# Full precision products on half arrays in the attention of a streaming encoder step

## The chip, the cores and the metric

The kernel runs on one core of a Trainium2 chip. The metric is the device time of one execution in microseconds (us): median 2494.75 of three runs, 2488.86 to 2495.19. Everything is float32, and the result must agree with a float32 reference.

Names used below: PE is TensorE (matmuls; PEld its weight loads), DVE VectorE, ACT ScalarE, POOL GpSimd, SP the queue that issues nearly all DMAs. PSUM is the memory that PE writes, in banks of 2 KB for each of 128 partitions; SBUF is the working memory.

## The reference

One layer of an encoder, for a prompt of 2048 tokens and for 8 samples of 16 tokens. Cut to the part that the change touches, the attention of the prompt over its own and the two previous chunks of 64 keys (8 query heads, 2 key heads, 64 wide):

```python
def band_attend(q, k, v, mask, sinks):
    s = jnp.einsum('bnlkgd,bnskd->bnkgls', q, k, preferred_element_type=jnp.float32) * (A_HEAD_DIM ** -0.5)
    if mask is not None:
        s = jnp.where(mask, s, -jnp.inf)
    sink = sinks.astype(jnp.float32).reshape(A_KV_HEADS, A_GROUP)[None, None, :, :, None, None]
    mx = jnp.maximum(jnp.max(s, axis=-1, keepdims=True), sink)
    p = jnp.exp(s - mx)
    p = p / (jnp.sum(p, axis=-1, keepdims=True) + jnp.exp(sink - mx))
    o = jnp.einsum('bnkgls,bnskd->bnlkgd', p.astype(v.dtype), v, preferred_element_type=jnp.float32)
    return o.astype(v.dtype)

def trunk_layer(...):
    qm, km, vm, om, ip, fp, qa, ka, va = split_in(x @ w_in)
...
    hm, C1, n1, m1 = mlstm_chunkwise(qm, km, vm, logi, logf, C0, n0, m0, mchunk)
...
        ha = swa_prompt(qa, ka, va, attn_sinks)
...
    mix = jnp.concatenate([hm, ha], axis=-1) @ w_out
    h = layer_norm(DEEPNORM_ALPHA * x + mix, ln1_g, ln1_b)
    f, conv_rows = conv_ffn(h, conv_prev, w_up, w_conv, b_conv, w_down)
    y = layer_norm(DEEPNORM_ALPHA * h + f, ln2_g, ln2_b)
```

## The kernel before

The tokens are 17 tiles of 128: tiles 0 to 15 the prompt, tile 16 all samples. Work runs in three stages. First the input projection (`i_block`, five blocks of up to four tiles) and the output projection with the first norm (`o_block`); then the up projection with its convolution (`f_ups`); then the down projection (`f_downs`). The last two use a saving scheme of seven products for eight and aren't touched.

**Products in split form.** A PE product of the type float32r goes at full rate but keeps fewer bits. So most operands are split by `split` (line 200): ACT copies the value to a float32r tile (hi, line 202) and DVE subtracts it from the value (lo, line 203). `mm3` (line 205) then makes three products: hi x hi (line 207), hi x lo (208, 209). A product whose operands are float32 is made in full precision and appears in the trace as two matmul records.

**Chains between dense work.** The projections of blocks are dense streams of products of 512 or 264 columns (PSUM tile `dps`). The mLSTM, the attention and the sample tile are three chains (`m_chain`, `a_chain`, `t_sample`), written as generators. `Chains.weave` (line 170) walks through the dense stream and adds up its cost in ns; when a chain is due, it lets it issue its next piece. A piece ends with `yield cost, delay`: cost is what the piece adds to that sum, delay how much later the next piece is due. So the yields set the order of PE's instructions, which stands as written. The order of the other engines is made by the compiler's scheduler.

**The attention of a tile** (`swa`, line 782), before the change:

- `swa_load` (760) loads q (`qa`) and k with v (`kva`, one buffer), and transposes q and k on PE into the banks `pq` and `pk`.
- q, k and v are split (lines 790 to 792): `qh`/`ql`, `kringh`/`kringl`, and `vring`, which holds for each key head the 64 hi columns and the 64 lo columns of v beside each other. The rings hold three tiles of keys.
- Scores: a key head has its 64 dimensions on one half of PE's rows (partitions 0 to 63, or 64 to 127). For each key head in turn, and for two pairs of query heads (`j0`), a bank `psc` is filled by two times three products of 256 keys. DVE adds the mask and reduces to the maximum (`amx`, line 815), while copying to `sc`.
- Softmax: small DVE steps (817 to 824, `aes`, `asm`), eight exponentials on ACT (822), the division as a product on POOL (825).
- Values: per key head, the probabilities are transposed on PE (`ppt`, line 835), split into `pth` and `ptl`, and multiplied: the 128 columns hi and lo of `vring` as weights, `pth` and `ptl` as moving operand of 512 columns (lines 842, 843; bank `ppo`). ACT copies one half of `ppo` to `mixa` (845), DVE adds the other (846).

The mLSTM's pieces share PSUM with these: score bank `pscore` (672), key transposes `pkt` (683), gate banks `pe` (654, 664; read on ACT by `wi` and on DVE by `dt`), `pemt` (585), `pnum` and `pcu` (745 to 753), and `pht` (721), the transposed output, which ACT copies to `mixm` (723) after DVE, POOL and ACT have normed it (`hn`, `ms`).

**PSUM.** `self.bank` (line 483) takes from a pool of five banks (`tps`) for all three chains. A new tile waits on PE for the last reader of the bank that it is given. As PE's order is fixed, all that stands behind it in PE's queue waits too.

The sample's chain uses the tags `qh`, `ql`, `pth`, `ptl` for its own buffers.

Of the kernel before, what the change touches and what calls it, by code (L numbers as in the profile page):

```python
# [18 lines left out]
DB = 8  # L19
DS = 16  # L20
# [11 lines left out]
RING = 3  # L32
# [157 lines left out]
class Prog:  # L190
# [295 lines left out]
    def t_setup(self):  # L486
        nc, a, tp = self.nc, self.a, self.tp

        def ld(n):
            t = self.one("k_" + n, list(a[n].shape))  # L490
            nc.sync.dma_start(t, a[n])
            return t
        nc.sync.dma_start(self.ident, a["ident"])
        self.gb = ld("gb")
        self.mcau = ld("mcau")
        self.mblk = ld("mblk")
        self.mswa = ld("mswa")
# [284 lines left out]
    def swa(self, t):  # L782
# [21 lines left out]
        scs = []  # L804
        for kvh in range(2):
            rs = slice(64 * kvh, 64 * kvh + 64)
            sink = self.sink[:, 4 * kvh:4 * kvh + 4]
            sc = self.work("sc", [P, 4, 2 * P], bufs=2)
            mx, es, sm = [self.work(n, [P, 4], bufs=2) for n in ("amx", "aes", "asm")]
            for j0 in (0, 2):  # L810
                ps = self.bank([P, 2, 2, P], "psc")
                for j in range(2):
                    self.mm3(ps[:, j, :nk], qh[rs, j0 + j], ql[rs, j0 + j], self.kh[rs, sel], self.kl[rs, sel], True, True)
                for j in range(2):
                    V.tensor_tensor_reduce(out=sc[:, j0 + j, :N], in0=ps[:, j, :nk].rearrange("p a b -> p (a b)"), in1=mask, scale=1.0, scalar=-3e38,
                                           op0=ALU.add, op1=ALU.max, accum_out=mx[:, j0 + j:j0 + j + 1])
# [9 lines left out]
            scs.append(sc)  # L826
        yield 2600, 7500
        for kvh in range(2):
            rs = slice(64 * kvh, 64 * kvh + 64)
            sc = scs[kvh]  # L830
            pth, ptl = self.work("pth", [P, 2, 512], F32R), self.work("ptl", [P, 2, 512], F32R)
            for kt in range(nk):
                pp = self.bank([P, 512], "ppt")
                for j in range(4):
                    nc.tensor.transpose(pp[:, j * P:(j + 1) * P], sc[:, j, kt * P:(kt + 1) * P], self.ident)
                self.split(pth[:, kt], ptl[:, kt], pp)
            yield 860, 3000

            po = self.bank([P, 512], "ppo")
            for kt in range(nk):  # L840
                w = self.vv[:, slots[kt], kvh].rearrange("p a d -> p (a d)")
                nc.tensor.matmul(po, w, pth[:, kt], start=kt == 0, stop=False)
                nc.tensor.matmul(po, w, ptl[:, kt], start=False, stop=kt == nk - 1)
# [7 lines left out]
    def t_sample(self):  # L851
# [43 lines left out]
        for j in range(2):  # L895
            ps = self.bank([P, 2, 129], "pnum")
            for i in range(2):
                h = 2 * j + i
                cn = self.work(("pth", "ptl")[h % 2], [P, DB, 129], name="cns")
# [8 lines left out]
                for i3, b0 in enumerate((0, 3, 6)):  # L908
                    nb = min(3, DB - b0)
                    vw = self.work(("qh", "ql")[i3 % 2], [P, nb, 129], name="vws")  # L910
# [13 lines left out]
    def swa_sample(self):  # L924
# [6 lines left out]
        qs = self.work("qh", [P, DB, 64], name="qs")  # L931
        V.tensor_copy(qs.rearrange("p b (j l) -> p j b l", j=4), pq.rearrange("p j (b l) -> p j b l", b=DB))
        ks = self.work("ql", [P, P], name="ks")
# [6 lines left out]
        for half in range(2):  # L940
# [5 lines left out]
            vn = self.work("ptl", [DS, HB, P], name="vn")  # L946
# [23 lines left out]
            pts = self.work("pth", [P, 2, HB, P], name="pts")  # L970
# [560 lines left out]
```

## Time and profile before

| | us |
|---|---|
| median of three runs | 2494.75 |
| their lowest and highest | 2488.86, 2495.19 |
| the profiled execution | 2496.35 |
| its span, first to last instruction | 2494.6 |
| PE busy | 2395.8 (96%) |
| DVE busy | 1865.9 (75%) |
| ACT busy | 1205.2 (48%) |
| POOL busy | 467.2 (19%) |
| mean granted clock of PE | 0.984 |

The profile is of one execution. Times are from the start of the span. Matmuls are pipelined, and the end of one is modelled, so two records overlap; what a product costs in a stream is the time from its start to the next one's. "Idle before" or a wait names the engine that waited, and which instruction's end released it. The clock is the share of full speed that PE was granted.

The prompt's attention and mLSTM run from about 220 us to 910 us, woven into the projections; the sample tile comes before them, and the feed-forward part after some 1060 us.

### The profile page before, as it was taken

The page shows a single profiled execution, that of the slowest core. Times are in us where ns is not written, and L with a number is a line of the kernel's source. Part 1 is how long each engine was busy: PE and PEld are TensorE (multiplying, and loading weights), DVE is VectorE, ACT ScalarE, POOL GpSimd, SP SyncE. Part 2 cuts the span into 40 slices and gives each one's busy share as a digit, 9 for nine tenths or more (in the row PEclk, how much of TensorE's full clock was granted, in tenths as well). Part 3 has the DMA queues.
Part 4 walks back from the last instruction along what each step waited for, and adds up shares of the span by engine and source line. Part 5 has one row for each costly group of instructions (what it writes and reads, how often), then busy time and mean ns, then how long its engine had stood idle before and what let it go on. Part 6 is the DMA issues. An engine that isn't in the chain of part 4 may idle for free.

```text
span 2494.6 us, 36890 instructions
## 1 busy us (share of the span) xinstructions
PE 2395.8 (96%) x12922; PEld 2131.1 (85%) x12922; DVE 1865.9 (75%) x3244; ACT 1205.2 (48%) x2170; POOL 467.2 (19%) x486
## 2 busy tenths in 40 slices
PE   8999999999989899989999999999999999999998
PEld 8777778878887777789999999999999978778776
DVE  5656777487588887888788876678766677796897
ACT  4323445344355543555555545555544544444553
POOL 1211332132143434310000000002000010220300
PEclk9999999999998999999999999999999999999999
DMA  8886744544556567667777789886998876656653
GB/s 268 306 275 221 249 128 136 174 125 136 176 163 204 174 205 261 212 227 271 288 279 264 264 301 315 314 304 223 326 300 262 267 267 205 232 188 203 219 185 108
DMA packets 277117, 575.28 MB, mean 231 GB/s; under 512 B 45300, under 2 KB 122204, under 8 KB 276932
## 3 DMA queue, kind: packets, MB, share of 16 engines
q1 hardware_dynamic: 275204, 566.64, 67.3%
q0 software_dynamic: 1728, 6.29, 0.7%
q8 instruction: 102, 1.67, 0.3%
q14 instruction: 83, 0.68, 0.1%
HBM read 419.06 MB, written 153.78 MB: 230 GB/s over the span
## 4 chain that ended last, share of the span: by engine, by line
PE 54%; DVE 10%; issue 4%; DMA 3%; ACT 3%; POOL 2%; SPq 0%; DVEq 0%; ACTq 0%; POOLq 0%
PE dps L1240 16%; PE fup L1240 15%; PE fht L1437 5%; PE dps L1437 5%; PE fup L1437 5%; PE dps L207 2%; PE dps L209 2%; PE dps L208 2%; DVE wlo L203 2%; DMA zf<-cc 1%; ACT cc L1286 1%; DVE cc L1288 1%; DVE hl L203 1%; PE fht L1112 0%; POOL ymix L1028 0%
## 5 line engine op out<-in xcount | busy, mean ns | idle before, releaser
L1240 PE MATMUL fup<-hh,uw 128*128 128x384 f32 (+1 forms) x1848 | 483.6, 330 | 10.8 <-ACT u L1265 3.5
L1240 PE MATMUL dps<-hh,uw 128*128 128x384 f32 (+1 forms) x1848 | 481.7, 329 | 7.4 <-ACT u L1265 5.1
L203 DVE TENSOR_TENSOR wlo<-wraw,whi 128x1024 fp32r<-128x1024 f32 (+3 forms) x289 | 349.0, 1215 | 143.8 <-ACT whi L202 137.2
L202 ACT CAST whi<-wraw 128x1024 fp32r<-128x1024 f32 (+3 forms) x289 | 281.8, 981 | 310.4 <-PE dps L1437 94.0
L1240 PEld LDWEIGHTS fup<-hh,uw 128*128 128x128 f32 x1848 | 331.8, 189 | 13.9 <-ACT u L1265 4.7
L1240 PEld LDWEIGHTS dps<-hh,uw 128*128 128x128 f32 x1848 | 330.6, 188 | 9.6 <-ACT u L1265 6.6
L1288 DVE SCALAR_TENSOR_TENSOR cc<-u,cw,cc 128x768 f32<-128x768 f32 (+1 forms) x264 | 252.6, 977 | 110.6 <-ACT cc L1286 108.2
L207 PE MATMUL dps<-whi,xh 128*128 128x512 f32 (+1 forms) x816 | 317.3, 389 | 0.0
L209 PE MATMUL dps<-whi,xl 128*128 128x512 f32 (+1 forms) x816 | 310.5, 380 | 2.3 <-DVE xl L349 2.3
L208 PE MATMUL dps<-wlo,xh 128*128 128x512 f32 (+1 forms) x816 | 310.5, 380 | 2.1 <-DVE wlo L203 2.0
L1240 PE MATMUL fup<-hl,uw 128*128 128x384 f32 (+1 forms) x924 | 303.7, 329 | 1.4 <-DVE hl L203 1.4
L1240 PE MATMUL dps<-hl,uw 128*128 128x384 f32 (+1 forms) x924 | 302.7, 328 | 0.0
L1286 ACT ACTIVATE cc<-u,cw 128x768 f32<-128x768 f32 (+1 forms) x132 | 129.6, 997 | 117.7 <-DVE u L1279 58.1
L209 PEld LDWEIGHTS dps<-whi,xl 128*128 128x128 f32 x816 | 155.1, 190 | 34.1 <-DVE xl L349 2.7
L208 PEld LDWEIGHTS dps<-wlo,xh 128*128 128x128 f32 x816 | 155.7, 191 | 31.4 <-DVE wlo L203 2.9
L207 PEld LDWEIGHTS dps<-whi,xh 128*128 128x128 f32 x816 | 155.8, 191 | 30.1 <-ACT xh L348 0.4
L1240 PEld LDWEIGHTS fup<-hl,uw 128*128 128x128 f32 x924 | 174.4, 189 | 1.6 <-DVE hl L203 1.6
L1240 PEld LDWEIGHTS dps<-hl,uw 128*128 128x128 f32 x924 | 173.9, 188 | 0.0
L1437 PE MATMUL fup<-whi,fu 128*128 128x512 f32 x484 | 159.6, 402 | 6.4 <-DVE yacc L1466 4.4
L1437 PE MATMUL dps<-whi,fu 128*128 128x512 f32 x440 | 149.0, 395 | 0.0
L1280 POOL COPY u<-prev 128x4 f32<-128x4 f32 x66 | 45.3, 687 | 465.2 <-DVE cc L1288 449.9
L1437 PE MATMUL fht<-whi,fu 128*128 128x512 f32 x396 | 132.1, 396 | 0.2 <-DVE yacc L1466 0.2
(289 smaller groups left out, 4598.7 us busy)
## 6 DMA issues: line engine op xcount, KB each, us to landing
uw<-zw SPq DMA_DIRECT2D x176, 512.0 KB, 4.7
zw<-uw SPq DMA_DIRECT2D x88, 512.0 KB, 2.9
wv<-wup SPq DMA_DIRECT2D x66, 512.0 KB, 5.6
wraw<-wtm SPq DMA_DIRECT2D x60, 512.0 KB, 4.8
wraw<-zt SPq DMA_DIRECT2D x60, 512.0 KB, 4.2
wraw<-wdn SPq DMA_DIRECT2D x45, 512.0 KB, 4.0
wraw<-wqk SPq DMA_DIRECT2D x40, 512.0 KB, 5.0
wraw<-wo SPq DMA_DIRECT2D x40, 512.0 KB, 4.8
```

Source lines behind the costliest of these rows:

```text
L202: nc.scalar.copy(hi, src)
L203: nc.vector.tensor_sub(lo, src, hi.bitcast(F32))
L207: mm(out, ah, bh, start=start, stop=False)
L208: mm(out, ah, bl, start=False, stop=False)
L209: mm(out, al, bh, start=False, stop=stop)
L1240: mm(ps, l[:, k], r[:, k], start=s in (1, 7) and k == 0 and i == 0, stop=k == 3 and i == 2, skip_group_check=True)
L1280: nc.gpsimd.tensor_copy(u[:, :, 0:2], self.prev[:, :, j])
L1286: S.activation(c[:, v], u[:, v, 2:2 + n], AF.Identity, bias=w[3], scale=w[2])
L1288: V.scalar_tensor_tensor(c[:, v], u[:, v, i:i + n], w[i], c[:, v], op0=ALU.mult, op1=ALU.add)
L1437: mm(ps, l[:, k, c], r[:, k], start=s in (1, 4, 7) and u == 0 and k == 0 and i == 0, stop=u == nu - 1 and k == n - 1 and i == 2, skip_grou ...
```

## The change

Products of the prompt's attention are made in full precision from unsplit operands, and the array is used in halves.

- The operands: q, k, v and the probabilities are no longer split. q and k are copied by ACT from PSUM to float32 tiles (`q`, `kk`); v is read straight from `kva`, which has three buffers now and serves as the ring; the probabilities are copied by ACT alone (`pth`, two buffers).
- Scores: two rounds (`j0` 0 and 2) with a `yield 1200, 1000` between them. In each, two banks, one for each key head, are filled by four products; the heads take turns, so that consecutive products lie on the lower and the upper half of PE's rows. The softmax of both key heads comes after the second round.
- Values: a loop over key blocks. The probabilities of both key heads are transposed and copied; one step later two products follow, one for each key head, with 64 columns of weights: head 0 writes partitions 0 to 63 of one bank `ppo`, head 1 partitions 64 to 127. One ACT copy takes the bank to `mixa`; DVE's addition is gone.
- In the sample's chain only the tags of buffers change: `ql` becomes a second buffer of `qh`, `ptl` one of `pth`.

```diff
@@ -511,8 +511,8 @@
                 t = self.one(f"{n}{i}", sh, F32R)
                 nc.vector.tensor_copy(t, src)
                 l.append(t)
-        self.kh, self.kl = [self.one(n, [P, RING, P], F32R) for n in ("kringh", "kringl")]
-        self.vv = self.one("vring", [P, RING, 2, 2, 64], F32R)
+        self.kk = self.one("kring", [P, RING, P])
+        self.kv = {}
         self.C = self.work("C", [P, MH, 129], bufs=2)
         nc.vector.memset(self.C, 0.0)
         self.mc = self.one("mc0", [MH, 1])
@@ -761,7 +761,7 @@
         nc = self.nc
         qa = self.work("qa", [P, 512])
         nc.sync.dma_start(qa, self.zqa[t])
-        kv = self.work("kva", [P, 256])
+        kv = self.work("kva", [P, 256], bufs=3)
         nc.sync.dma_start(kv, self.zkv[t])
         pq = self.bank([P, 4, P], "pq")
         for j in range(4):
@@ -786,10 +786,10 @@
         if t == NPT - 1:
             nc.sync.dma_start(self.a["kv_p"], kv)
         r = t % RING
-        qh, ql = self.work("qh", [P, 4, P], F32R), self.work("ql", [P, 4, P], F32R)
-        self.split(qh, ql, pq)
-        self.split(self.kh[:, r], self.kl[:, r], pk)
-        self.split(self.vv[:, r, :, 0], self.vv[:, r, :, 1], kv[:, P:].rearrange("p (a d) -> p a d", a=2))
+        q = self.work("qh", [P, 4, P], bufs=2)
+        nc.scalar.copy(q, pq)
+        nc.scalar.copy(self.kk[:, r], pk)
+        self.kv[r] = kv
         if t == 0:
             slots, nk = [0], 1
             mask = self.mswa[:, 0, P:]
@@ -801,19 +801,25 @@
         N = nk * P
         yield 550, 4500
         mix = self.work("mixa", [P, 4, P])
-        scs = []
+        scs = [self.work("sc", [P, 4, 2 * P], bufs=2) for _ in range(2)]
+        mxs = [self.work("amx", [P, 4], bufs=2) for _ in range(2)]
+
+        for j0 in (0, 2):
+            ps = [self.bank([P, 2, 2, P], "psc") for _ in range(2)]
+            for j in range(2):
+                for kvh in range(2):
+                    rs = slice(64 * kvh, 64 * kvh + 64)
+                    nc.tensor.matmul(ps[kvh][:, j, :nk], q[rs, j0 + j], self.kk[rs, sel], start=True, stop=True)
+            for kvh in range(2):
+                for j in range(2):
+                    V.tensor_tensor_reduce(out=scs[kvh][:, j0 + j, :N], in0=ps[kvh][:, j, :nk].rearrange("p a b -> p (a b)"), in1=mask, scale=1.0,
+                                           scalar=-3e38, op0=ALU.add, op1=ALU.max, accum_out=mxs[kvh][:, j0 + j:j0 + j + 1])
+            if j0 == 0:
+                yield 1200, 1000
         for kvh in range(2):
-            rs = slice(64 * kvh, 64 * kvh + 64)
             sink = self.sink[:, 4 * kvh:4 * kvh + 4]
-            sc = self.work("sc", [P, 4, 2 * P], bufs=2)
-            mx, es, sm = [self.work(n, [P, 4], bufs=2) for n in ("amx", "aes", "asm")]
-            for j0 in (0, 2):
-                ps = self.bank([P, 2, 2, P], "psc")
-                for j in range(2):
-                    self.mm3(ps[:, j, :nk], qh[rs, j0 + j], ql[rs, j0 + j], self.kh[rs, sel], self.kl[rs, sel], True, True)
-                for j in range(2):
-                    V.tensor_tensor_reduce(out=sc[:, j0 + j, :N], in0=ps[:, j, :nk].rearrange("p a b -> p (a b)"), in1=mask, scale=1.0, scalar=-3e38,
-                                           op0=ALU.add, op1=ALU.max, accum_out=mx[:, j0 + j:j0 + j + 1])
+            sc, mx = scs[kvh], mxs[kvh]
+            es, sm = [self.work(n, [P, 4], bufs=2) for n in ("aes", "asm")]
             V.scalar_tensor_tensor(mx, mx, 0.125, sink, op0=ALU.mult, op1=ALU.max)
             V.tensor_sub(es, sink, mx)
             nc.scalar.activation(es, es, AF.Exp)
@@ -823,28 +829,24 @@
             V.tensor_add(sm, sm, es)
             V.reciprocal(sm, sm)
             nc.gpsimd.tensor_mul(sc[:, :, :N], sc[:, :, :N], sm.rearrange("p (h o) -> p h o", o=1).to_broadcast([P, 4, N]))
-            scs.append(sc)
-        yield 2600, 7500
-        for kvh in range(2):
-            rs = slice(64 * kvh, 64 * kvh + 64)
-            sc = scs[kvh]
-            pth, ptl = self.work("pth", [P, 2, 512], F32R), self.work("ptl", [P, 2, 512], F32R)
-            for kt in range(nk):
+        yield 1200, 7500
+
+        po = pts = None
+        for kt in range(nk + 1):
+            new = self.work("pth", [P, 2, 512], bufs=2) if kt < nk else None
+            for kvh in range(2) if kt < nk else ():
                 pp = self.bank([P, 512], "ppt")
                 for j in range(4):
-                    nc.tensor.transpose(pp[:, j * P:(j + 1) * P], sc[:, j, kt * P:(kt + 1) * P], self.ident)
-                self.split(pth[:, kt], ptl[:, kt], pp)
-            yield 860, 3000
-
-            po = self.bank([P, 512], "ppo")
-            for kt in range(nk):
-                w = self.vv[:, slots[kt], kvh].rearrange("p a d -> p (a d)")
-                nc.tensor.matmul(po, w, pth[:, kt], start=kt == 0, stop=False)
-                nc.tensor.matmul(po, w, ptl[:, kt], start=False, stop=kt == nk - 1)
-            m = mix[rs].rearrange("p a b -> p (a b)")
-            nc.scalar.copy(m, po[64 - 64 * kvh:128 - 64 * kvh])
-            V.tensor_add(m, m, po[rs])
-            yield 900, 0
+                    nc.tensor.transpose(pp[:, j * P:(j + 1) * P], scs[kvh][:, j, kt * P:(kt + 1) * P], self.ident)
+                nc.scalar.copy(new[:, kvh], pp)
+            if kt:
+                po = po or self.bank([P, 512], "ppo")
+                for kvh in range(2):
+                    w = self.kv[slots[kt - 1]][:, P + 64 * kvh:P + 64 * kvh + 64]
+                    nc.tensor.matmul(po[64 * kvh:64 * kvh + 64], w, pts[:, kvh], start=kt == 1, stop=kt == nk)
+            pts = new
+            yield (860 if kt < nk else 0) + (1400 if kt else 0), 0 if kt == nk else 1500 if kt else 3000
+        nc.scalar.copy(mix.rearrange("p a b -> p (a b)"), po)
         self.mix_out(t, 4, mix)
...
```

More of the change, by code (lines that the diff above doesn't have):

```diff
@@ L898, in t_sample @@
                 h = 2 * j + i
-                cn = self.work(("pth", "ptl")[h % 2], [P, DB, 129], name="cns")
+                cn = self.work("pth", [P, DB, 129], bufs=2, name="cns")
                 nc.sync.dma_start(cn, a["cn0"][:, h])
@@ L909, in t_sample @@
                     nb = min(3, DB - b0)
-                    vw = self.work(("qh", "ql")[i3 % 2], [P, nb, 129], name="vws")
+                    vw = self.work("qh", [P, nb, 129], bufs=2, name="vws")
                     V.tensor_mul(vw, v1[:, h:h + 1, :].to_broadcast([P, nb, 129]), last(dt, h, b0, nb))
@@ L929, in swa_sample @@
         nc.sync.dma_start(a["kv_s"], kv)
-        qs = self.work("qh", [P, DB, 64], name="qs")
+        qs = self.work("qh", [P, DB, 64], bufs=2, name="qs")
         V.tensor_copy(qs.rearrange("p b (j l) -> p j b l", j=4), pq.rearrange("p j (b l) -> p j b l", b=DB))
-        ks = self.work("ql", [P, P], name="ks")
+        ks = self.work("qh", [P, P], bufs=2, name="ks")
         V.tensor_copy(ks, pk)
@@ L945, in swa_sample @@
             nc.sync.dma_start(vc, a["vc"][:, bs])
-            vn = self.work("ptl", [DS, HB, P], name="vn")
+            vn = self.work("pth", [DS, HB, P], bufs=2, name="vn")
             nc.sync.dma_start(vn, self.zkv[t][half * 64:half * 64 + 64, P:].rearrange("(b l) e -> l b e", b=HB))
@@ L969, in swa_sample @@
             yield 2700, 6500
-            pts = self.work("pth", [P, 2, HB, P], name="pts")
+            pts = self.work("pth", [P, 2, HB, P], bufs=2, name="pts")
             pp = self.bank([P, HB, P], "ppt")
```

## The prediction

> **What bounds the kernel now.** I read three things in this order: busy time by stretch, the waits of TensorE (PE) in the stretch that the change touches, and that stretch instruction by instruction.
>
> Busy time by stretch (start:end, length, then busy time of PE, PEld, DVE, ACT, POOL, the granted clock, the DMA share, GB/s):
>
> ```profile
> 0.00:220.00 220.00, 201.69 (x1090) 171.25 (x1091) 123.54 (x242) 74.61 (x138) 39.24 (x46) 0.97 0.80 270
> 220.00:910.00 690.00, 650.32 (x3581) 543.94 (x3580) 513.74 (x1406) 331.46 (x801) 220.59 (x184) 0.97 0.53 171
> 910.00:2494.00 1584.00, 1543.80 (x8255) 1415.87 (x8253) 1228.59 (x1597) 799.14 (x1231) 207.38 (x256) 0.99 0.73 251
> ```
>
> The prompt's attention (first score product at 226 us, last value product at 907 us) lies in the middle row. There PE is busy 650.3 of 690 us, so 39.7 us are lost to waits; the clock of 0.97 costs about 0.03 x 690 = 21 us more. DVE is at 74%, ACT at 48%. So an edit counts by what it does to PE's own work, and by how it moves those 39.7 + 21 us. The last row isn't touched: PE's order is the same there.
>
> PE's waits between 220 and 910 us (who waited, for whom, total us, times, longest):
>
> ```profile
> PE pkt L683 <- DVE amx L815: 6.9, 3, 2.7
> PE pemt L585 <- ACT mixm L723: 5.7, 3, 2.1
> PE pht L721 <- ACT hn L710: 5.2, 4, 2.9
> PE ppo L843 <- DVE ptl L203: 4.5, 4, 1.3
> PE psc L207 <- DVE dt L656: 2.7, 1, 2.7
> PE ppt L835 <- DVE asm L823: 2.6, 1, 2.6
> ```
>
> These are mostly waits for one of the five PSUM banks that the two chains share; the reader of the old contents is late. A wait of 2 us also costs clock, as the windows around 320, 506 and 690 us showed (0.57, 0.76 and 0.69).
>
> **The prices on PE.** One score visit, the one at 312 us (start, length, what):
>
> ```profile
> 311.54 0.40 PE L209 MATMUL dps<-xh,wlo 128*128 128x512 f32 x1
> 311.86 0.38 PE L207 MATMUL psc<-kringh,qh 64*128 64x256 f32 x1
> 312.09 0.28 PE L208 MATMUL psc<-kringl,qh 64*128 64x256 f32 x1
> ...
> 312.92 0.39 PE L207 MATMUL psc<-kringh,qh 64*128 64x256 f32 x2
> 313.15 0.29 PE L208 MATMUL psc<-kringl,qh 64*128 64x256 f32 x2
> 313.27 0.28 PE L209 MATMUL psc<-kringh,ql 64*128 64x256 f32 x2
> ...
> 314.53 0.50 PE L207 MATMUL dps<-xh,whi 128*128 128x512 f32 x1
> 314.87 0.40 PE L208 MATMUL dps<-xl,whi 128*128 128x512 f32 x1
> ```
>
> Matmuls overlap, so I count from start to start. Dense products of 512 columns follow each other by 0.23 us. The visit begins when the next dense product was due (311.54 + 0.23 = 311.77) and ends at 314.53; the dense step after it is 0.34 instead of 0.23. So a visit takes 2.76 + 0.11 = 2.87 us. Its 24 products fill 21 steps of 0.111, 2.34 us: where the first key head (rows 0 to 63) meets the second (rows 64 to 127), three products of each run at the same time (the x2 rows). The other 0.53 us is the price of going to half rows and back.
>
> A full precision product is two records. In the sample part four records of 128x387 (L913) take 133.62, 133.94, 134.27, 134.59: a step of 0.325 us, 0.84 ns a column. So 256 columns cost 2 x 0.215 = 0.43 us and 512 columns 2 x 0.43 = 0.86 us.
>
> **The change, part by part** (15 tiles with two key blocks, one with one).
>
> *Scores.* Removed: the visit of 2.87 us. Added: two visits of four full precision products, two per row half, in turn. The x2 rows show halves of rows at work together, and the sample's scores (full precision, heads in turn on two quadrants) start 13 ns apart. With that a visit is 0.53 + 2 x 0.43 = 1.39 us, two are 2.78: -0.1 us a tile. Without it 0.53 + 4 x 0.43 = 2.25, two 4.50: +1.6.
>
> *Value products.* Removed: eight products in the dense tiling, 8 x 0.233 = 1.87 us. Added: per key block one visit with one product per column half. No row shows two halves of columns at work at once. Bounds: together, 0.53 + 0.86 = 1.39, two 2.78 (+0.9 a tile); one after the other, 0.53 + 1.72 = 2.25, two 4.50 (+2.6). I take the first, since the nearest row is the pair of quadrants, which differ in columns as well as rows.
>
> Sum on PE: 15 x 0.8 = 12, and about 0.2 for the first tile: **+12 us**. Serial columns add 31 x 0.86 = 27 us, serial rows 31 x 0.86 = 27.
>
> The Trainium skill (TensorEngine Tiling, Key Properties) says that a change of tiling mode drains the engine; the 0.53 us agrees, and it speaks against this change, with four visits a tile for one.
>
> *Work taken from DVE and ACT.* Per tile DVE loses ql 0.68, kringl 0.28, vring 0.63, four ptl of 0.68 and two mixa adds of 0.68: 5.7 us, 16 x 5.7 = 90 of its 514 us. ACT loses vring (0.3, which stood waiting 28.7 us in all for kva to land) and one mixa copy of 0.58. None of this is PE's; it is worth nothing unless a wait shrinks. kva with three buffers is loaded ahead; its values are read straight from it, so no DMA is added.
>
> *Waits.* Scores now take two banks at a time, not four.
> - Block starts (pkt <- amx with pe and pemt behind it: 3.3 us at 319, 2.8 at 506, 2.1 at 690; 2.9 at 232). The last of four banks was read at 321.1, 9 us after the visit began, with DVE behind xl (1.78) and two wlo. Now four reductions of 0.35 are in the way, and the split of q (0.68) is gone. The order built for the changed kernel puts pscore, pkt and pe2 before the first reuse of these banks: 0.3 + 1.4 + 0.9 + 0.4 + 0.3 = 3.3 us of PE work. The second score visit waits for wi and emt instead, some 0.8 us. Four sites, 11.1 us now, 3.2 then: **-8 us**.
> - ptl (4.5) goes with the split; psc <- dt (2.7) and pk <- dt (1.9) lose their place in the order; ppt <- asm and pht <- hn (7.8) about halve, as more dense work stands before them: **-13 us**.
> - pemt <- mixm (5.7 at three sites) grows. ACT's order keeps mixm behind the eight exponentials (8 x 0.49 = 3.9 us). At 368 they began 4.9 us after the score visit ended. Now all eight reductions end before the first exponential, 1.1 us more, with a wlo of 0.8 between the two visits' reductions, and PE reaches pemt 6 us after the second visit instead of 8. I take 4.3 us per site: **+7 us**.
> - The clock follows the waits: 14 of 39.7 us fewer, in proportion 0.35 x 21: **-7 us**.
>
> Sum: +12 - 8 - 13 + 7 - 7 = **-9 us**. The profiled execution took 2496.35 us (span 2494.6 and 1.75 around it), above all three timed runs; taking 9 from the median 2494.75 gives **2486 us**.
>
> **Rivals.**
> 1. *The column halves run one after the other.* For it: no row with two; the sample's value products (L983, 64 columns, one half) only show 0.106 between the two records. Against it: the quadrants. Price +27: 2486 + 27 = 2513, slower. The Trainium skill (TensorE: Matmul & The Clock Gate, part 3) says weight loads overlap running matmuls only where the row group differs; halves of columns share all rows, so by that rule this rival follows. But the dense products also share all rows, and their loads (189 ns each) are hidden in steps of 233 ns, so the trace does not agree with it as worded; the same section reports 2.38 times for three column tiles.
> 2. *The mixm waits take back what the banks give.* pemt stands in line before dense work at three sites, and ACT's order is fixed. If a site costs 7 us and two clock windows, instead of 4.3 and one, that is 3 x (2.7 + 1.7) = 13 more, and 6 more if hn and asm keep theirs: 2486 + 19 = 2505, slower. It decides from 6 us a site on. For it: at 368 the exponentials ended 9 us after the visit. Against it: ql, kringl and vring no longer stand before them.
> 3. *Even.* PE's extra 12 us and the shorter waits cancel: with waits and clock down by 12 instead of 21, 2495. For it: waits move on to the next bank user easily with five banks.
> 4. *The row halves don't overlap* in full precision: +27, 2513. The sample's quadrants speak strongly against it.
>
> **How the numbers follow.** About 0.3% (7.5 us) is what a measurement of this kernel can tell from no change. Forecast 0.47 (its own range 2464 to 2487), even 0.20 (2488 to 2502), serial columns 0.18, mixm 0.11, serial rows 0.04. So faster 0.47, same 0.20, slower 0.33. The low end: mixm unchanged at 5.7 and another 5 us of waits gone (-12), the clock with them (-6), and 0.1 us less in each value visit, since loads of 64 columns are shorter (L983 134 ns against 188): -3, to 2465, and 1 for the scatter. The high end holds each serial case and 2 us more: 2515. Beyond it stay both at once, or one with rival 2.
>
> **What would show it.** In the changed profile: the two records of the second key head's score product start a few ns after the first's, and a visit is near 1.4 us; the value products of the two column halves likewise, with a step of 0.43 us (0.86 from pair to pair would be serial). PE's idle time between 220 and 910 us falls from 39.7 to 25 or so, amx and ptl leave its list, mixm leads it. The clock there goes from 0.97 to 0.98. I am wrong if the column halves start 0.86 us apart, if PE's idle time does not fall, or if time after 910 us changes.

## The result, and the profile after

| | before | after |
|---|---|---|
| median, us (19 runs each) | 2495.19 | 2499.85 |
| lowest and highest | 2487.6, 2505.37 | 2496.6, 2505.48 |
| profiled execution: span | 2494.6 | 2496.6 |
| PE idle, whole span (span less PE's busy time) | 98.8 | 104.0 |
| lost to the clock (span x (1 - mean granted clock)) | 39.9 | 37.4 |
| what is left: PE's own work at full clock | 2355.9 | 2355.2 |

The ratio is 1.002, with a 95% interval of 1.0012 to 1.0028: the changed kernel is 4.7 us slower, where 9 us faster was forecast. That is less than the 0.3% that the prediction took as no change, but the interval lies above 1.

The three lower rows are worked out from each profile's busy times and clock, and the clock has three digits, so a row is good to about 2 us; kernels below that make the same products differ by up to 5 us in the last row. They already say that PE's own work hardly changed and that idle time grew by 5 us. The clock of this one profile isn't typical: 0.985 is the highest of the changed kernel's 19 executions, whose median is 0.984, while the kernel before has a median of 0.985 or 0.986 in the runs beside each experiment. So over all executions the change also lost clock, and 0.001 of it is 2.5 us.

Busy time by stretch in the profile of the changed kernel (columns as before: PE, PEld, DVE, ACT, POOL, clock, DMA share, GB/s):

```profile
0.00:220.00 220.00, 202.59 (x1095) 172.06 (x1096) 124.57 (x243) 75.13 (x139) 42.06 (x46) 0.98 0.80 272
220.00:910.00 690.00, 643.78 (x3421) 504.73 (x3420) 431.75 (x1260) 311.53 (x765) 217.33 (x184) 0.96 0.52 169
910.00:2496.00 1586.00, 1546.20 (x8281) 1417.97 (x8279) 1231.16 (x1600) 802.35 (x1234) 207.38 (x256) 1.00 0.74 252
```

In the middle row PE is idle for 690 - 643.8 = 46.2 us, against 39.7 before. DVE has 82 us less to do there (90 were forecast), and PE's idle time grew all the same. PE's waits in that stretch:

```profile
PE ppt L840 <- POOL sc L831: 22.0, 15, 3.0
PE pe L654 <- DVE amx L815: 6.3, 3, 2.1
PE pemt L585 <- ACT mixm L723: 6.1, 2, 3.0
PE pe L664 <- POOL re L575: 5.6, 3, 2.7
PE ppt L840 <- DVE asm L829: 1.6, 1, 1.6
```

The waits for `ptl`, `dt` and `hn` (14.3 us before) are gone, and that for `asm` fell from 2.6 to 1.6. In their place stands one that was next to nothing before:

```profile
PE ppt L835 <- POOL sc L825: 0.5, 1, 0.5
```

Now the transposition of the probabilities (`ppt`) waits for the division on POOL (`sc`, line 831) for 22.0 us at 15 places. One of them, instruction by instruction (start, length, what, and in brackets the idle time before it and its releaser):

```profile
409.25 0.19 ACT L828 ACTIVATION_READ_ACCUMULATOR sc<-sc,amx 128x1 f32 x1
...
409.47 0.37 DVE L829 TENSOR_TENSOR asm<-asm,aes 128x4 f32<-128x4 f32 x1 [1.69 <-ACT sc L828]
...
409.87 0.18 DVE L830 RECIPROCAL asm<-asm 128x4 f32<-128x4 f32 x1
409.87 0.65 PE L840 MATMUL ppt<-ident,sc 128*128 128x128 f32 x4 [0.70 <-POOL sc L831]
...
410.19 1.89 POOL L831 TENSOR_TENSOR sc<-sc,asm 128x1024 f32<-128x1024 f32 x1 [0.38 <-ACT gates L413]
...
412.14 0.66 PE L840 MATMUL ppt<-ident,sc 128*128 128x128 f32 x4 [1.61 <-POOL sc L831]
```

At 409.87 PE transposes the first head's probabilities. ACT had the sums of the second head's last exponential at 409.44, DVE had the reciprocal at 410.05, and POOL then took 1.89 us for the division. PE stands 1.61 us, and all dense work with it, since its order is fixed. Before the change the first transposition piece held one head alone, with dense work between it and the second's.

The halves do work at the same time. A score visit and a value visit of the changed kernel, with the dense products around:

```profile
308.93 0.40 PE L209 MATMUL dps<-xh,wlo 128*128 128x512 f32 x1
309.25 1.13 PE L812 MATMUL psc<-kring,qh 64*128 64x256 f32 x8
310.32 0.51 PE L207 MATMUL dps<-xh,whi 128*128 128x512 f32 x1
310.66 0.40 PE L208 MATMUL dps<-xl,whi 128*128 128x512 f32 x1
```

```profile
339.96 1.08 PE L846 MATMUL ppo<-pth,kva 128*64 128x512 f32 x4
340.97 0.51 PE L207 MATMUL dps<-xh,whi 128*128 128x512 f32 x1
341.31 0.40 PE L208 MATMUL dps<-xl,whi 128*128 128x512 f32 x1
```

A score visit takes from 308.93 + 0.23 to 310.32, and 0.11 for the longer step behind it: 1.27 us (1.39 was forecast). A value visit takes 1.01 us to the next dense start, the same 0.11, and 0.09 of a longer entry: 1.21 us (also 1.39). The timeline puts records of a kind into one line; taken singly, the second half's record starts 6 to 7 ns after the first's in both (309.253 and 309.259, 340.441 and 340.447).

### The profile page after: what moved, and what is told of

It is laid out like the page before. It is cut to its first block, busy times and chain, and to the rows that moved or that the text cites. A ratio compares the mean times of both kernels' runs of the same rounds, so it can differ in the third digit from the quotient of the medians.

```text
span 2496.6 us, 36481 instructions
## 1 busy us (share of the span) xinstructions
PE 2392.6 (96%) x12794; PEld 2094.8 (84%) x12794; DVE 1787.5 (72%) x3102; ACT 1189.0 (48%) x2138; POOL 466.8 (19%) x486
## 4 chain that ended last, share of the span: by engine, by line
PE 65%; DVE 10%; ACT 4%; issue 4%; DMA 3%; POOL 3%; DVEq 0%; SPq 0%; POOLq 0%; ACTq 0%
PE dps L1242 17%; PE fup L1242 17%; PE fht L1439 5%; PE dps L1439 5%; PE dps L207 5%; PE dps L208 4%; PE dps L209 4%; PE fup L1439 4%; DVE wlo L203 2%; ACT sc L828 1%; PE ppo L846 1%; PE ppt L840 1%; DVE sc L815 1%; DVE hl L203 1%; POOL sc L831 1%
## 5 line engine op out<-in xcount | busy, mean ns | idle before, releaser
L207 PE MATMUL dps<-xh,whi 128*128 128x512 f32 (+2 forms) x320 | 126.0, 394 | 6.5 <-ACT xh L348 5.9
```

Source lines behind the costliest of these rows:

```text
L207: mm(out, ah, bh, start=start, stop=False)
```

## The experiments

The theory after the result (A): the waits that were saved were taken back by the new wait of `ppt` for the second head's division. Its rival (B): with an order fixed on PE, a wait that is removed turns up at the next place, so that no single wait costs what the list shows. Times are medians over the runs. Ratios are to the kernel before, run beside each experiment, with a 95% interval. A profiled execution can lie some us off its median.

**The new wait, from three sides.** First, the value step falls due later:

```diff
-        yield 1200, 7500
+        yield 1200, 11000
```

> The value step falls due 3.5 us later after the scores; nothing else changes. Theory A (the gain went into the new wait of the first transposition, line 840, for the second key head's division on POOL, 22.0 us at 15 sites between 220 and 910 us): that wait falls below 6 us, PE's idle time there from 46.2 to about 30, the clock loses less, and the time falls by 12 to 20 us to 2480-2488. Theory B (PE's own work is what the change costs, and a wait taken away at one place turns up at another): the wait leaves line 840 but idle time stays within 5 us of 46, and the time within 4 us of 2500.

Second, the first head's transposes become a piece of their own (the cost of the step is reduced by as much):

```diff
+                if kt == 0 and kvh == 0:
+                    yield 430, 4000
```

> The first head's transposes of the first key block become a piece of work of their own, so that TensorE needs only the first head's division at first and the second's later. Theory A (the wait for the second head's division took the gain): the 22.0 us at line 840 fall by half or more and the time by 6 to 12 us, to 2488-2494. Theory B (waits only move): 2496-2504. If the planner puts both pieces next to each other anyway, the wait stays near 22 and the run says nothing between A and B.

Third, the division goes from POOL to DVE:

```diff
-            nc.gpsimd.tensor_mul(sc[:, :, :N], ...)
+            V.tensor_mul(sc[:, :, :N], ...)
```

> The changed kernel with the softmax's division (line 831) on DVE instead of POOL. By a DVE row of the same shape (wlo, 128x1024, 1.28 us) it takes about 1.3 us instead of 1.9 and doesn't queue behind POOL's qk (1.3 us); DVE gains 16 x 2 x 1.3 = 42 us of work, half of what the change had taken off it. Theory A (the wait for the division took the gain): the 22.0 us at line 840 fall below 8, idle time of PE between 220 and 910 us by 8 or more, the time to 2488-2496. Theory B (a wait taken away turns up elsewhere, in the planner's fixed order): idle time stays within 4 us of 46.2 and the time is 2497-2502.

Measured: the later step 2495.3 us (ratio 0.9999, 0.9989 to 1.0008); the separate piece 2497.49 (1.0005, 0.9996 to 1.0014); the division on DVE 2490.46 (0.9984, 0.9973 to 0.9994). So the first takes back what was lost, and the third 4 us more. The later step's time lies between the ranges of A and B. The separate piece halved the wait (11.1 us) and stayed in B's range of times, and its interval overlaps that of the changed kernel, so a gain isn't shown there. The waits of the first (same view as above) show that B has its share:

```profile
PE pe L664 <- POOL re L575: 9.8, 4, 5.5
PE dps L208 <- DVE wlo L203: 7.6, 4, 2.4
PE pe L654 <- DVE amx L815: 7.1, 4, 2.1
PE ppt L840 <- POOL sc L831: 5.1, 2, 4.4
```

The wait fell from 22.0 to 5.1 us as A said, and idle time only from 46.2 to 43.6, as B said: `re` and `wlo` took its place. With the division on DVE the wait stayed on the list with DVE as its releaser (20.3 us at 11 places, where below 8 was expected), and idle time in the stretch fell by 4.7 us, to 41.5, between what A and B had named. Yet the time fell as A said. In the profiles PE was idle for 97.7 us over the whole span, not 104.0, and the clock was 0.987, not 0.985, worth 5 us; the two make the 11.4 us by which the spans differ. Part of that is chance: this profiled execution is the fastest of ten, and over all of them the median clock is 0.985, against 0.984, and the time 9.4 us shorter. Both together (`yield 1200, 11000`, and the division on DVE):

> The value step due 3.5 us later (as in the run before) and the division on DVE. There the later value step alone had taken the wait at line 840 from 22.0 to 5.1 us, but waits for POOL (re 9.8, qk 4.6) and for DVE (wlo 7.6) stood in its place, idle time was 43.7 and the time 2495.3. Theory A' (POOL's queue, in which both divisions stand, is what makes re and qk late too): the waits for re and qk fall below 8 us together, idle time below 38, the time to 2486-2492. Theory B (order alone): 2494-2499.

2489.49 us (0.9978, 0.9968 to 0.9988): the time is in the range of A', while idle time (39.7) and the waits for `re` (still 9.9) aren't. The waits for `qk` left the leading entries of the list. Against the division on DVE alone the time differs by 1 us, which the intervals don't tell from nothing.

**The two halves of the change, each alone.** First the scores of the changed kernel with the value products of the kernel before (the diff is against the changed kernel):

```diff
-        for kt in range(nk + 1):
...
+        for kvh in range(2):
...
+                self.split(pth[:, kt], ptl[:, kt], pp)
+            yield 860, 3000
...
+                nc.tensor.matmul(po, w, pth[:, kt], start=kt == 0, stop=False)
+                nc.tensor.matmul(po, w, ptl[:, kt], start=False, stop=kt == nk - 1)
```

> Scores of the changed kernel (full precision, row halves in turn), value products of the kernel before (split, dense tiling, head after head). PE's own work by the records: two score visits of 1.27 for one of 2.87 us, -0.3 us a tile, -5 in all. Theory A (the wait for the second head's division): the first transposition needs the first head alone, so the wait at line 840's counterpart is under 8 us, and the time is 2484-2492. Theory B (the scores in turn themselves make the rest late, whoever reads them): the wait stays over 15 us and the time is 2496-2504.

Then the scores and softmax of the kernel before with the value products of the changed kernel (the diff is again against the changed kernel):

```diff
+        self.split(qh, ql, pq)
+        self.split(self.kh[:, r], self.kl[:, r], pk)
...
+                    self.mm3(ps[:, j, :nk], qh[rs, j0 + j], ql[rs, j0 + j], self.kh[rs, sel], self.kl[rs, sel], True, True)
...
+        yield 2600, 7500
```

> Scores and softmax of the kernel before (split, head after head), value products of the changed kernel (full precision, column halves). PE's own work by the records: two value visits of 1.21 for 1.87 us of dense products, +0.55 us a tile, +8 in all. Theory A (the first transposition piece needs both heads' divisions, whatever the scores' order): the wait at line 840 is 12 us or more and the time is 2500-2510. Theory B (the order of the scores is what makes the divisions late): the wait is under 8 us and the time 2490-2498.

Scores alone: 2498.95 us (1.001, 0.9999 to 1.002). Values alone: 2493.53 (0.9993, 0.9979 to 1.0008). PE's own work, worked out as in the first table, is 2349.3 and 2360.5, so -6.6 and +4.6 against the kernel before. The prices of the records (-5 and +8) come out in sign, and in size within what that row is good for; the two add up to -2.0, where both together gave -0.7. The times went the other way round: the half that costs PE work was, if anything, faster, and the half that saves it was not. For the scores, theory A had the wait right (4.9 us, under 8) and the time wrong (2484 to 2492). In the list of PE's waits others had come:

```profile
PE pe L654 <- DVE amx L815: 9.9, 4, 3.5
PE ppo L849 <- DVE ptl L203: 8.6, 9, 2.3
PE pemt L585 <- ACT mixm L723: 6.5, 2, 3.3
PE ppt L841 <- POOL sc L831: 4.9, 3, 2.0
```

For the values alone B was right in both: the wait at the transposition was 7.9 us, not 12 or more, and the time within 2490 to 2498. So neither the step that needs both heads nor the scores in turn make the 22 us alone (4.9 and 7.9); together they do. With the scores in turn, both heads' softmax is behind all reductions; with the first step needing both, PE stands until the later one is divided.

What that costs is another matter, and PE's idle time (whole span less busy time, one profile each) says it better than the list. It is 98.8 us before, 103.0 with the scores alone, 92.9 with the values alone and 104.0 with both. If the two halves simply added up, both together would have 97.1. So where the list shows 22.0 us, the meeting of the two halves costs about 7 us of idle time, as far as single profiles can tell, and the scores alone bring 4.2. The clock goes the same way: its median over ten runs is 0.983 with the scores alone and 0.9855 with the values alone, against 0.985 for the kernel before beside them.

**All scores in one visit.**

```diff
-        for j0 in (0, 2):
-            ps = [self.bank([P, 2, 2, P], "psc") for _ in range(2)]
...
-            if j0 == 0:
-                yield 1200, 1000
+        ps = [[self.bank([P, 2, 2, P], "psc") for _ in range(2)] for _ in range(2)]
...
+        for kvh in range(2):
+            for j in range(4):
+                V.tensor_tensor_reduce(...)
```

> All sixteen score products of a tile in one visit on four banks, as the kernel before took them, but in full precision and in turn on the row halves; the reductions of the first head come first, so its softmax starts after four reductions, not after eight. One change of tiling less a tile: 15 x 0.5 = 7 us less on PE. Theory C (two visits apart make both heads' softmax late, which is what the in-turn scores cost): the wait at line 840 falls below 12 us and the time is 2486-2495. Rival (four banks at once bring back the waits for banks): waits for amx rise from 6.3 to over 12 us and the time is 2496-2504.

2508.84 us (1.0052, 1.0035 to 1.0069): the rival's case, and slower than its range. PE's own work fell by 2.8 us, not 7, its waits for `amx` rose to 13.5, and that for the division was 17.3, not below 12. Theory C isn't tested by this run. It takes the first head's four reductions first, but the softmax of both heads still stands behind all eight, in the kernel and in DVE's order in every tile; in the kernel before, the first head's softmax began after four or five. One place of the timeline shows what the four banks do:

```profile
306.74 2.00 PE L811 MATMUL psc<-kring,qh 64*128 64x256 f32 x16
309.47 1.05 PE L672 MATMUL pscore<-qk 128*128 128x128 f32 x8
315.78 1.09 PE L683 MATMUL pkt<-ident,qk 128*128 128x128 f32 x4 [5.26 <-DVE amx L814]
```

Four of five banks are held by scores, DVE comes to read them only 8.1 us after the visit began, and the next piece that wants a bank stands 5.26 us. So two rounds with two banks, as the change has them, are worth their second entry.

**What the halves of columns are worth.** Both heads' products on the same half, each into its own bank, with two copies on ACT instead of one:

```diff
-                po = po or self.bank([P, 512], "ppo")
+                po = po or [self.bank([64, 512], "ppo") for _ in range(2)]
...
-                    nc.tensor.matmul(po[64 * kvh:64 * kvh + 64], w, ...)
+                    nc.tensor.matmul(po[kvh], w, ...)
```

> The changed kernel with both key heads' value products on the same half of the columns, each head into a bank of its own, with two copies out on ACT instead of one. It measures what the column halves at the same time are worth. The traces show the second half's records 6 to 7 ns after the first's, so each of 31 visits should grow from 1.21 us by one full precision pass of 512 columns, 0.43 less the 0.04 that a step costs more with both halves at work, and there are two products a head pair: if a pass of one half takes 0.86 us (two records of 0.43), PE gains 31 x 0.86 - 31 x 0.1 = 24 us and the time is 2516-2530. If the halves gained nothing, the time stays at 2497-2503.

2539.83 us (1.018, 1.0161 to 1.0199), beyond the expected 2516 to 2530. The busy time of the value products alone from 220 to 960 us (PE, PEld, clock, DMA share, GB/s), first of the changed kernel and then of this one:

```profile
220.00:960.00 740.00, 33.44 (x124) 6.13 (x124) 0.97 0.54 174
```

```profile
220.00:960.00 740.00, 62.42 (x124) 14.76 (x124) 0.96 0.50 161
```

The same 124 records take 29 us more, and one visit goes from 1.01 to 1.86 us:

```profile
344.34 1.93 PE L846 MATMUL ppo<-pth,kva 128*64 128x512 f32 x4
346.20 0.50 PE L207 MATMUL dps<-xh,whi 128*128 128x512 f32 x1
```

That is 31 x 0.85 = 26.4 us by start times, the price that the first rival had (27); the time grew by 40, since idle time (104.0 to 111.6) and the clock (0.985 to 0.982) came on top. The second bank and the second copy may have their part in that; no run separates them. The Trainium skill (TensorE: Matmul & The Clock Gate, Part 3) says that weight loads overlap running products only where the groups of rows differ, and gives 2.38 times for three products on column tiles. Here the halves share all rows and still start 6 to 7 ns apart, so the trace agrees with the second statement and not with the first as a limit on what runs together.

**Towards a faster version.** Three runs show what is a matter of order and what of engines. The later value step with the division and `re` on DVE:

```diff
-        nc.gpsimd.tensor_tensor(re[0:4], ...)
-        nc.gpsimd.tensor_tensor(re[96:100], ...)
+        nc.vector.tensor_tensor(re[0:4], ...)
+        nc.vector.tensor_tensor(re[96:100], ...)
```

> Value step due 3.5 us later, division on DVE, and now the two products that build re (4x512, lines 574 and 575, 1.3 us each on POOL) on DVE too. In the run without the last step the waits for re were 9.9 us at 4 sites, idle time between 220 and 910 us 39.7 and the time 2489.5. Theory A (the readers of the softmax and of re are late because POOL's own work stands in series with them): the waits for re fall below 5 us, idle time to 33-36, time 2481-2487. Theory B (it only moves on, to amx, wlo or sd): idle time 38-42, time 2487-2492.

2486.91 us (0.9965, 0.9954 to 0.9977), at the upper end of A's range; idle time (37.5) and the waits for `re` (5.4) just missed theirs. Then the separate piece of the first head, `yield 1200, 9000`, and division and `re` on DVE:

> First head's transposes as a piece of their own, value step due 1.5 us later, division and re on DVE. Theory A: the wait at line 840, 11.1 us with the separate piece alone, falls below 5; idle time 32-37; time 2481-2487. Theory B: idle time 39 or more, time 2488-2494.

2481.55 us (0.9944, 0.9929 to 0.9958): 14 us under the kernel before, idle 32.4 in the stretch, as A said. And the same with division and `re` left on POOL:

> The changed kernel with the first head's transposes as a piece of their own and the value step due 1.5 us later; division and re stay on POOL. If the two orders of the planner do most of it: 2484-2490, wait at line 840 below 8 us. If the place of the division does most of it: 2492-2498, and waits for POOL (sc, re, qk) of over 15 us in all.

2486.02 us (0.9965, 0.9952 to 0.9977), and in its list of waits that at line 840 is down to 0.8 us:

```profile
...
PE pnum L746 <- POOL qk L736: 6.0, 3, 2.6
PE pe L664 <- POOL re L575: 5.8, 3, 2.9
...
PE ppt L840 <- POOL sc L831: 0.8, 1, 0.8
```

So the order of two pieces brings 14 of the 18 us between 2499.85 and 2481.55. The division and `re` on DVE bring some 4.5, which isn't clear, since the intervals of the two ratios overlap.

**Does the gain need the change?** The same moves on the kernel before (its heads are separate pieces already) and on each half; in all three `re` is made on DVE as above.

```diff
-            nc.gpsimd.tensor_mul(sc[:, :, :N], ...)
-        yield 2600, 7500
+            V.tensor_mul(sc[:, :, :N], ...)
+        yield 2600, 9000
```

> The kernel before with the same three moves that brought the changed kernel to 2481.6 us, as far as it has them: division and re on DVE, value step due 1.5 us later (its heads are separate pieces already). It asks whether the gain needs the change. Theory A (the moves pay because the change took 82 us of work off DVE, and because only its order makes the divisions late): DVE, 514 us busy of 690 already, gets 42 + 22 us more, and the time is 2492-2502. Rival (they pay in any order): 2478-2486.

The scores alone, with `yield 1200, 9000`:

> Scores of the changed kernel, value products of the kernel before, with division and re on DVE and the value step due 1.5 us later. By PE's own work (5 to 6 us less than the kernel before in the first comparison) and with the waits equal, 2478-2482 against 2485.2 of the kernel before with the same moves. If the scores in turn make their readers late whatever the order (they cost 3 us in the first comparison), 2485-2491.

The values alone, with `yield 2600, 9000` and the first head's piece (`yield 430, 4000`):

> Scores of the kernel before, value products of the changed kernel, with the first head's transposes as a piece of their own, division and re on DVE and the value step due 1.5 us later. By PE's own work (5 to 6 us more than the kernel before) and with the waits equal, 2488-2493. If the lighter reading of the value products (no split of the probabilities) shortens waits as in the first comparison, where this part was 2 us faster, 2480-2485.

| ratio to the kernel before | orders as given | with the moves |
|---|---|---|
| neither half | 1 | 0.9968 (0.9954 to 0.9982) |
| scores alone | 1.001 (0.9999 to 1.002) | 0.9965 (0.9955 to 0.9974) |
| values alone | 0.9993 (0.9979 to 1.0008) | 0.9928 (0.9913 to 0.9944) |
| both | 1.002 (1.0012 to 1.0028) | 0.9944 (0.9929 to 0.9958) |

The first expectation's theory was wrong and its rival right: the kernel before gained 10 us as well (2485.2), with DVE at 540 of 690 us. The scores alone (2484.99) came out at the lower edge of the case that they make their readers late whatever the order, and the values alone (2475.55) were faster than both of their ranges. The moves pay in any order, and the change needs them: by the ratios they bring 0.32% to the kernel before and 0.76% to the changed one. With them, the value products on column halves are worth 0.2 to 0.4% (0.9965 to 0.9944, with intervals that touch, and 0.9968 to 0.9928, with intervals apart; 2475.55 us is the fastest kernel of this study). The scores on row halves bring nothing that shows. Yet by PE's own work it is the value products that cost (2365.4 against 2359.3) and the scores that save. The values win by waits, and by the clock that goes with them. PE's idle time over the whole span (one profile each), and the median clock of all runs:

| | idle, us, orders as given | clock | idle, us, with the moves | clock |
|---|---|---|---|---|
| neither half | 98.8 | 0.985 | 95.8 | 0.987 |
| scores alone | 103.0 | 0.983 | 98.3 | 0.985 |
| values alone | 92.9 | 0.9855 | 83.5 | 0.9895 |
| both | 104.0 | 0.984 | 86.9 | 0.986 |

In both orders the scores on row halves add idle time and cost clock; the values take idle time away, except beside the scores in the orders as given. The busy time of the fastest version between 220 and 910 us, and PE's waits there:

```profile
220.00:910.00 690.00, 664.33 (x3675) 533.06 (x3675) 489.59 (x1384) 326.01 (x781) 128.83 (x127) 0.99 0.55 176
```

```profile
PE ppt L834 <- DVE sc L825: 6.2, 1, 6.2
PE pnum L745 <- issue: 5.0, 4, 1.9
PE dps L208 <- DVE wlo L203: 3.0, 4, 1.5
PE pemt L585 <- ACT wi L666: 2.9, 4, 1.4
```

PE is idle for 25.7 us there, against 37.9 in the kernel before with the moves and 39.7 without. One run in between shows that the place of the division alone does not do it for this half: the values alone with only the division moved,

> The value products in column halves with the scores of the kernel before (2493.5 us, wait for the division on POOL 7.9 us), and the division on DVE. Theory A: that wait falls below 3 us, the time to 2486-2492. Theory B: the wait moves, and the time is 2492-2497.

took 2495.6 us (1.0009, 0.9996 to 1.0021), B's case: the wait went from 7.9 to 6.4 us and the rest moved.

What stays open is why the scores in turn bring this idle time, so that they gain nothing although PE's work falls. With the moves the longest waits of their profile are for `amx` at the starts of blocks (9.3 us at 3 places) and one of 6.1 for the division. No run took these away one at a time, and none let the first head's softmax start before the second head's reductions, as it did in the kernel before.

## Why the prediction failed, point by point

The step that failed is the waits' second item: that the waits of `ppt` for `asm` and of `pht` for `hn` "about halve". For `hn` and for the split's waits the direction was right; the five waits of the item lost 15 us (13 forecast). For `ppt` the sign was wrong, since another producer took the place of `asm`. I priced the wait that stood there before, and didn't ask what the transposition needs now: both heads' divisions in one piece, after eight reductions, eight exponentials and two divisions of 1.9 us on POOL. The parts were all on the page, and I used the late exponentials for `mixm`, one line further down, but not here. In its place the list shows 22.0 us at 15 places. The later step (wait 5.1) and the later, separate pieces (0.8) show that this wait can be removed, and also that its price can't be read off the list: the first brought 4.6 us and the second 14, but nearly the same moves bring 8 to 10 us to the kernel before, which hasn't got this wait. By idle time it costs about 7 us (104.0 for both halves, 97.1 if they added up). The rest of the lost idle time and clock comes with the scores alone, and its cause stays open.

- *PE's own work, +12.* Mis-sized: -0.7 by the table, +3 by the records (2 x 1.27 + 2 x 1.21 = 4.96 us a tile against 2.87 + 1.87 = 4.74, 15 tiles). The overhead of a visit is 0.41 and 0.35 us over its passes of 0.86, not 0.53; that price came from a visit of 24 products in split form.
- *The halves overlap*: right for rows and columns. The first rival would have cost about 40 us, not 27, by the run on one half of the columns.
- *Waits for banks at block starts, -8.* Nothing came. 11.1 us before; now `amx` and `re` there make 11.9. I counted four reductions of 0.35 us, but not what stands ahead of them in DVE's queue. After the score visit at 309.25 us the timeline has (DVE and PE):

```profile
314.81 1.18 DVE L564 CAST me<-mc 4x128 fp32r<-4x128 f32 x1
315.97 0.50 PE L664 MATMUL pe<-re,me 100*128 100x512 f32 x1 [2.66 <-POOL re L575]
316.03 0.28 DVE L565 TENSOR_TENSOR me<-mc,me 4x128 fp32r<-4x128 f32 x1
...
316.51 1.23 DVE L203 TENSOR_TENSOR wlo<-wraw,whi 128x1024 fp32r<-128x1024 f32 x1 [0.20 <-PE pe L664]
...
317.66 0.42 DVE L815 CUSTOM_DVE_ANT_0 sc<-psc,k_mswa 128x256 f32<-128x256 f32 x1
...
318.57 0.76 PE L654 MATMUL pe<-re,ae 100*128 100x512 f32 x1 [2.10 <-DVE amx L815]
```

  DVE works through the rows of the mLSTM's gates (`me` is the last of them) and a `wlo`, and comes to the first reduction 8.4 us after the scores began; the bank is free only then. And `re`, which POOL makes out of the same rows, is late for the piece before.
- *`pemt` for `mixm`, +7.* 5.7 to 6.1: nothing.
- *The clock, -7.* It was to follow the waits, and did, the other way: 0.97 to 0.96 in the stretch, and 0.985 to 0.984 in the medians of all runs. That is a loss of about 2.5 us where 7 were to be gained.
- *What would show it.* Idle time rose instead of falling to 25, which was named as the sign of being wrong. The time after 910 us holds what was still to be done there: the last value product starts at 912.4 us, not 907.1. The third rival (2495 us) is nearest in time, but by luck: PE's 12 us didn't come, the waits didn't shorten, and the new wait is for an operand, not for one of the five banks. The second rival had the late exponentials right and looked for them at `mixm`.

## What to carry to other kernels

When a change makes one step need several results at once, price its wait anew from the chain of the last of them; the wait that the old profile shows there says nothing. Where an engine's order is fixed, a saved wait is worth its length only if the next reader is early; move the due times together with the change before judging it, and give the old kernel the same moves before praising it. Work taken from an engine that isn't the bottleneck (DVE, -82 us) need not bring anything: the largest entry of PE's waits for DVE's `amx` was 6.9 us before and 6.3 after. And read idle time beside the list of waits, in each half of a change alone: here the list named a wait of 22.0 us, and the idle time priced it at about 7.

## What the runs showed of the hardware

Two things were not expected. Full precision products on one half of the columns cost more than their passes: 26 us of work became 40 us of time in the run above, the rest in waits and clock. And the clock falls after idle time, not in it. By stretches of 3.4 us around the block start above, where PE waited 2.66 and 2.10 us with half a microsecond of work between (columns as in the table of stretches):

```profile
314.40:317.80 3.40, 0.50 (x1) 0.19 (x1) 3.13 (x7) 0.60 (x1) 1.82 (x2) 1.00 0.90 304
317.80:321.20 3.40, 2.63 (x9) 2.15 (x10) 2.45 (x10) 0.80 (x2) 1.06 (x1) 0.60 0.30 82
321.20:324.60 3.40, 3.40 (x10) 2.23 (x8) 2.82 (x16) 0.87 (x5) 0.00 (x0) 0.50 0.00 0
```

PE is fully busy in the last row and gets half the clock, so the waits of 4.8 us cost about 3 us more. In the trace's record of the clock it is half from 318.47 us on, for 6.8 us; in the 3.4 us before that PE was idle for 2.9 us, at full clock. Up to 1100 us this profile has 13 such stretches, of 3.4 or 6.8 us. In the 3.4 us ahead of 12 of them PE was idle for 1.7 to 3.0 us, in one or several gaps; ahead of one, at 216 us, it wasn't idle, and why the clock fell there stays open. In 3.4 us from 690.5 on PE was idle for 1.9 us and kept its clock. The Trainium skill (TensorE: Matmul & The Clock Gate, HAM oscillation) names idle gaps of more than about 3.4 us as those to avoid; here neither gap ahead of the fall was that long (2.66 and 2.10 us), so the trace puts the point lower.
